# The last six blocks of a gated feed-forward's down product, as Strassen's seven products of half size

## The chip, the cores and the metric

The kernel runs on one core of a Trainium2 chip. The metric is the device time of one execution in microseconds (us). In the names below TensorE (PE) multiplies matrices and VectorE (DVE), ScalarE (ACT), GpSimd (POOL) and SyncE (SP) do the rest; SP issues nearly all transfers from HBM.

## The reference

Two decoder blocks follow each other on 512 tokens of width 1024: latent attention and two feed-forwards with windowed attention between them, and then a second block with a convolution and dilated attention. Its end is what matters here:

```python
h = rmsnorm(x, g_ffn[i])
gate = causal_dwconv3(h @ w_gate[i], ffn_conv_w[i], ffn_conv_b[i])
x = x + (jax.nn.silu(gate) * (h @ w_up[i])) @ w_down[i]        # 2816 features
ple_gate = jax.nn.sigmoid(rmsnorm(x, g_ple[i]) @ w_ple_gate[i])
x = x + ple_gate * (p[i].astype(x.dtype) @ w_ple_proj[i])
```

All is float32. 2816 features are 22 blocks of 128.

## The kernel before

Every float32 operand of a product is split in a high and a low part of a rounded format (`split`, lines 118 to 120: ScalarE casts the high part, line 119, VectorE subtracts it, line 120). `mm3` (lines 202 to 204) then does a product as three matmuls: high by high, high by low, low by high. One matmul has 128 rows of a stationary operand and up to 512 columns.

The down product of 16 of the 22 blocks is done in two passes of `down_steps`, eight blocks each. A pass cuts its hidden activations (A, 1024 features by 512 tokens) in four parts, the weights (B, 1024 by 1024) in four, and forms Strassen's seven products of half size (in Winograd's form). Sums of A and B parts are VectorE's (`a_sum`, line 915; `b_sum`, line 924), then they are split (`a_op`, `b_op`). A product fills two PSUM banks `R[0]`, `R[1]`, one for each 128 tokens of its half of the tokens. The result is added to `x` by VectorE (line 885), in one to three places. Three pairs of banks serve the seven products: the fourth product goes on in the banks of the first (`R1`), the fifth in those of the third (`R2`), the sixth in those of the second (`R3`), the seventh in `R2` again, so each of these comes behind the additions that read those banks. `down_steps` is a generator, and between its steps stand the gate and up products of later features (`gated`, 48 matmuls each), so that TensorE has other work while the sums are made.

The last six blocks' activations are split as they arise (lines 1608 and 120), and their down product is the plain one: `gemm_tm` for columns 0 to 511 and `gemm_tm_t` for 512 to 1023, four groups of 128 tokens, six blocks, three matmuls: 72 and 72. In between the second pass and it stands a small projection, `w_ple_proj` (48 matmuls), whose results ScalarE copies out of PSUM (line 1681).

When the last column half of a token group is added (`ev_down`), `to_ple` forms the last norm of these 128 tokens: a multiplication by the gain (VectorE, line 1637), squares with a running sum (ScalarE, line 1642), a square root and a few one-column operations. The transposes of that group (`put_t`, line 447) are put off by `put_off` and come after some `tick`s or when the gate product asks for them (`need`). Then `w_ple_gate` is multiplied, the end of the kernel.

The framework schedules: each engine gets its own order of instructions, from the program's order, given priorities (`tc.high_priority`) and its own cost model. On the chip each engine works in its order and waits for semaphores.

## Time and profile before

| what | us |
|---|---|
| median of 3 runs | 1692.81 (1691.04 to 1693.84) |
| the profiled execution | 1690.43 |
| its span in the profile | 1688.6 |
| TensorE busy | 1669.5 |
| VectorE busy | 1111.0 |
| ScalarE busy | 829.3 |

The span is from the first to the last instruction of the profiled execution. A line number is that of the source, often a helper's, so the names of the tiles tell more: `wr` and `wq` are raw weights, `wh` and `wl` their high and low parts, `aop` a split A operand, `r` the banks of a small product, `tm` and `tt` those of plain products, `pt` those of transposes, `hr` raw activations, `xth` and `xtl` transposed activations. Matmuls are pipelined: a row's duration is longer than the distance from the start of one to that of the next.

### The profile page before, as it was taken

The numbers are of one execution on the slowest core, as the hardware profiler recorded it, in microseconds if no ns is written. First come the engines' busy times: TensorE is split into PE (matmuls) and PEld (weight loads), VectorE is DVE, ScalarE is ACT, GpSimd is POOL, SyncE is SP. The second block draws the span as 40 slices with busy tenths as digits, with TensorE's granted clock in tenths as the row PEclk, the third lists the DMA queues.
The fourth block names the chain that finished last, engine by engine and source line by source line (L and its number), as shares of the span: only waits on it lengthen the run. The fifth ranks groups of instructions, "written<-read, shape, count | busy, mean of one in ns | idle before, by whom it ended". The sixth has DMA issues, their size and how long they took to land.

```text
span 1688.6 us, 21336 instructions
## 1 busy us (share of the span) xinstructions
PE 1669.5 (99%) x8239; PEld 1384.7 (82%) x8239; DVE 1111.0 (66%) x1938; ACT 829.3 (49%) x1416; POOL 25.6 (2%) x43
## 2 busy tenths in 40 slices
PE   8999999999999999999999999999999999999998
PEld 8777898888888877798888888988779888888887
DVE  5876648576846578738586846556765567577463
ACT  4665445444543578445444545444854343344442
POOL 0000000000001110000000000001000000000000
PEclk9999999999999999999999999999999999999999
DMA  5213244333132323413333143133352323422321
GB/s 181 69 46 130 88 150 119 100 100 100 50 125 87 101 63 119 156 50 101 101 99 100 50 126 111 39 125 99 100 187 63 88 76 99 125 63 63 113 88 63
DMA packets 125015, 165.22 MB, mean 98 GB/s; under 512 B 9385, under 2 KB 80322, under 8 KB 124914
## 3 DMA queue, kind: packets, MB, share of 16 engines
q1 hardware_dynamic: 119072, 150.03, 28.2%
q10 hardware_dynamic: 4626, 10.94, 1.9%
q0 software_dynamic: 1216, 2.89, 0.8%
q8 instruction: 65, 1.06, 0.3%
q14 instruction: 36, 0.29, 0.1%
HBM read 160.95 MB, written 2.88 MB: 97 GB/s over the span
## 4 chain that ended last, share of the span: by engine, by line
PE 94%; DVE 3%; ACT 1%; DMA 1%; issue 0%; SPq 0%; ACTq 0%; DVEq 0%
PE up L202 8%; PE up L204 8%; PE up L203 8%; PE r L202 6%; PE r L204 6%; PE r L203 6%; PE tt L203 3%; PE tt L204 3%; PE tt L202 3%; PE tm L202 2%; PE tm L203 2%; PE fm L202 2%; PE tm L204 2%; PE fm L203 2%; PE fm L204 2%; PE gp L204 2%
## 5 line engine op out<-in xcount | busy, mean ns | idle before, releaser
L120 DVE TENSOR_TENSOR wl<-wr,wh 128x1024 fp32r<-128x1024 f32 (+5 forms) x219 | 222.8, 1032 | 168.8 <-ACT wh L119 167.7
L119 ACT CAST wh<-wr 128x1024 fp32r<-128x1024 f32 (+5 forms) x219 | 193.6, 898 | 273.1 <-PE up L203 118.0
L202 PE MATMUL up<-xth,wh 128*128 128x512 f32 x608 | 236.5, 389 | 0.0
L203 PE MATMUL up<-xtl,wh 128*128 128x512 f32 x608 | 236.5, 389 | 0.0
L204 PE MATMUL up<-xth,wl 128*128 128x512 f32 x608 | 236.5, 389 | 0.0
L120 DVE TENSOR_TENSOR wl<-wq,wh 128x1024 fp32r<-128x1024 f32 x112 | 136.4, 1223 | 101.0 <-ACT wh L119 100.9
L119 ACT CAST wh<-wq 128x1024 fp32r<-128x1024 f32 x112 | 118.0, 1054 | 159.2 <-PE r L204 82.4
L204 PE MATMUL r<-wh,aop 128*128 128x512 f32 x448 | 174.3, 389 | 0.0
L202 PE MATMUL r<-wh,aop 128*128 128x512 f32 x448 | 174.3, 389 | 0.0
L203 PE MATMUL r<-wl,aop 128*128 128x512 f32 x448 | 174.3, 389 | 0.0
L204 PEld LDWEIGHTS up<-xth,wl 128*128 128x128 f32 x608 | 114.1, 188 | 23.8
L203 PEld LDWEIGHTS up<-xtl,wh 128*128 128x128 f32 x608 | 114.1, 188 | 23.6
L202 PEld LDWEIGHTS up<-xth,wh 128*128 128x128 f32 x608 | 114.1, 188 | 23.5
L204 PEld LDWEIGHTS r<-wh,aop 128*128 128x128 f32 x448 | 84.1, 188 | 17.5
L203 PEld LDWEIGHTS r<-wl,aop 128*128 128x128 f32 x448 | 84.1, 188 | 17.4
L202 PEld LDWEIGHTS r<-wh,aop 128*128 128x128 f32 x448 | 84.1, 188 | 17.4
L885 DVE SCALAR_TENSOR_TENSOR x<-x,r 128x512 f32<-128x512 f32 x144 | 92.5, 684 | 5.4 <-PE r L204 5.4
L120 DVE TENSOR_TENSOR aop<-hr,aop 128x1024 fp32r<-128x1024 f32 x56 | 67.0, 1221 | 21.5 <-ACT aop L119 21.5
L924 DVE TENSOR_TENSOR wq<-wq,wq 128x1024 f32<-128x1024 f32 x64 | 76.2, 1223 | 6.4 <-DMA wq<-in_w_down_dram 3.9
L202 PE MATMUL gp<-xth,wh 128*128 128x512 f32 x160 | 62.3, 389 | 0.0
L203 PE MATMUL gp<-xtl,wh 128*128 128x512 f32 x160 | 62.3, 389 | 0.0
L204 PE MATMUL gp<-xth,wl 128*128 128x512 f32 x160 | 62.2, 389 | 0.0
(426 smaller groups left out, 3561.4 us busy)
## 6 DMA issues: line engine op xcount, KB each, us to landing
wr<-in_mlp_w_up_dram SPq DMA_DIRECT2D x64, 512.0 KB, 3.8
wq<-in_mlp_w_down_dram SPq DMA_DIRECT2D x48, 512.0 KB, 4.3
wr<-in_w_in_dram SPq DMA_DIRECT2D x24, 512.0 KB, 3.6
wr<-in_w_gate_dram SPq DMA_DIRECT2D x22, 512.0 KB, 3.7
wr<-in_w_up_dram SPq DMA_DIRECT2D x22, 512.0 KB, 3.6
wr<-in_mlp_w_down_dram SPq DMA_DIRECT2D x16, 512.0 KB
wq<-in_w_down_dram SPq DMA_DIRECT2D x16, 512.0 KB, 7.8
wr<-in_mla_w_o_dram SPq DMA_DIRECT2D x8, 512.0 KB, 3.7
```

The source lines that it names most:

```text
L119: turned["hi"] = nc.scalar.copy(out=hi, in_=src).ins
L120: return nc.vector.tensor_tensor(out=lo, in0=src, in1=hi.bitcast(F32), op=ALU.subtract)
L202: nc.tensor.matmul(o, lhsT=sh, rhs=mh, start=start, stop=False, skip_group_check=True)
L203: nc.tensor.matmul(o, lhsT=sh, rhs=ml, start=False, stop=False, skip_group_check=True)
L204: nc.tensor.matmul(o, lhsT=sl, rhs=mh, start=False, stop=stop, skip_group_check=True)
L885: nc.vector.scalar_tensor_tensor(out=x[:, t, cs], in0=x[:, t, cs], scalar=alpha, in1=pb, op0=ALU.mult, op1=ALU.add)
L924: nc.vector.tensor_tensor(out=out[:, ks, :], in0=a[:, ks, :], in1=b[:, ks, :], op=op)
```

## The change

`down_steps` takes a number of blocks per half, `nk` (4 before, now also 3), and a function `fin` that it calls when a token group is complete. The last six blocks' activations are kept raw in two tiles of three blocks, and their down product is a third pass with `nk=3`, in place of the two plain products. No gate or up product is left to stand between its steps. The first half of the gate weights is loaded and split after the third to the sixth step (`ahead2.one()`); before, it came with the second plain product. In all passes the sums of A for the last two products now stand ahead of both, and with `fin` these two are swapped, so that token groups 0 and 1 are complete one product before 2 and 3. A `tick` follows each small product.

```diff
-    def down_steps(mb, wd, row, ra, rb, alpha, after=None):
+    def down_steps(mb, wd, row, ra, rb, alpha, after=None, nk=4, fin=None):
...
-            B[r, h] = q = mb.tile([P, 4, S], F32, tag="q", name=f"wq_{n_big[0]}")
-            for i in range(2):
-                nc.sync.dma_start(out=q[:, 2 * i:2 * i + 2, :],
-                                  in_=krows(wd, row + r * 4 + 2 * i, 2, h * 512, 512))
+            B[r, h] = q = mb.tile([P, nk, S], F32, tag="q", name=f"wq_{n_big[0]}")
+            for k0 in range(0, nk, 2):
+                kn = min(2, nk - k0)
+                nc.sync.dma_start(out=q[:, k0:k0 + kn, :], in_=krows(wd, row + r * nk + k0, kn, h * 512, 512))
...
         def product(R, a, b, start):
-            for i, (wh, wl) in enumerate(b):
+            for k0, kn, wh, wl in b:
                 for tb in range(2):
-                    for k in range(2):
+                    for k in range(kn):
                         ts_ = slice(tb * P, (tb + 1) * P)
-                        kk = 2 * i + k
+                        kk = k0 + k
                         mm3(R[tb], (a[:, 0, kk, ts_], a[:, 1, kk, ts_]), (wh[:, k, :], wl[:, k, :]),
-                            start and kk == 0, kk == 3)
+                            start and kk == 0, kk == nk - 1)
+            tick()
 
-        def add(R, th, h, al=1.0):
+        def add(R, th, h, al=1.0, last=False):
             for tb in range(2):
                 ev_add(x, al)(h, 2 * th + tb, R[tb])
+                if last and fin:
+                    fin(2 * th + tb)
...
-        b = b_op(B21)
-        product(R3, a22, b, False)
         a_sum(A12, A12, A22, ALU.subtract)
         s4 = a_op(A12)
-        add(R3, 1, 0)
-        yield
-        b = b_op(B22)
-        product(R2, s4, b, False)
-        add(R2, 0, 1)
-        yield
+        rest = [(R3, a22, B21, 1, 0), (R2, s4, B22, 0, 1)]
+        for R, a, src, th, h in reversed(rest) if fin else rest:
+            b = b_op(src)
+            product(R, a, b, False)
+            add(R, th, h, last=True)
+            yield
...
-                n_big[0] += 1
-                a = ff.tile([P, S], F32, tag="a", name=f"a_{n_big[0]}")
-                nc.vector.tensor_tensor(out=a, in0=Y.pop((gr, m)), in1=banks[m], op=ALU.mult)
-                split(*H[gr * 2 + m - 16], a)
+                M = gr * 2 + m
+                c, k = (M // 4, M % 4) if M < 16 else (4 + (M - 16) // 3, (M - 16) % 3)
+                if k == 0:
+                    RAW[c] = big("hr", F32)
+                turned["y", gr] = nc.vector.tensor_tensor(out=RAW[c][:, k, :], in0=Y.pop((gr, m)), in1=banks[m],
+                                                          op=ALU.mult).ins
...
-        gemm_tm(H, wd[16 * P:22 * P, :], [LO], ev_down)
-        ahead2 = gemm_tm_t(H, wd[16 * P:22 * P, :], [HI], ev_down, 1,
-                           nxt=lambda: ahead_tm(io["w_ple_gate_2"][0], 0, 512))
+        with pool("fl", 4) as fl:
+            ahead2 = Ahead([(krows(io["w_ple_gate_2"][0], k, 2, 0, 512), 2, 512, None) for k in range(0, 8, 2)])
+            for i, _ in enumerate(down_steps(fl, wd, 16, RAW.pop(4)[:, 0:3, :], RAW.pop(5)[:, 0:3, :], 1.0, nk=3,
+                                             fin=to_ple)):
+                if 2 <= i < 6:
+                    ahead2.one()
```

VectorE's order, before: what stands behind the small projection's four splits. `wl_1890` to `wl_1893` are parts of the down weights, `wl_1895` to `wl_1897` of the gate weights, `tm_...` banks of the plain product.

```order
L120 TENSOR_TENSOR wl_1890_13673<-wr_1890_13671,wh_1890_13672 128x1024
L120 TENSOR_TENSOR wl_1891_13707<-wr_1891_13705,wh_1891_13706 128x1024
L120 TENSOR_TENSOR wl_1892_13713<-wr_1892_13711,wh_1892_13712 128x1024
L120 TENSOR_TENSOR wl_1895_13728<-wr_1895_13726,wh_1895_13727 128x1024
L120 TENSOR_TENSOR wl_1893_13719<-wr_1893_13717,wh_1893_13718 128x1024
L120 TENSOR_TENSOR wl_1896_13734<-wr_1896_13732,wh_1896_13733 128x1024
L120 TENSOR_TENSOR wl_1897_13740<-wr_1897_13738,wh_1897_13739 128x1024
L1648 TENSOR_TENSOR x1_375_1792<-x1_375_1792,tm_1884_13607 128x512
L1648 TENSOR_TENSOR x1_375_1792<-x1_375_1792,tm_1885_13608 128x512
L1648 TENSOR_TENSOR x1_375_1792<-x1_375_1792,tm_1886_13609 128x512
L1648 TENSOR_TENSOR x1_375_1792<-x1_375_1792,tm_1887_13610 128x512
```

VectorE's order now, at the place where the fourth of the seven new products is due. `wq_1880` and `wq_1877` are the weights' parts B21 and B11, `r_1884` and `r_1885` the banks of the first product, `wl_1905` and `wl_1906` the split of B11.

```order
L924 TENSOR_TENSOR wq_1880_13599<-wq_1880_13599,wq_1877_13590 128x1024
L924 TENSOR_TENSOR wq_1880_13599<-wq_1880_13599,wq_1877_13590 128x512
L924 TENSOR_TENSOR wq_1877_13590<-wq_1878_13593,wq_1877_13590 128x1024
L924 TENSOR_TENSOR wq_1877_13590<-wq_1878_13593,wq_1877_13590 128x512
L885 SCALAR_TENSOR_TENSOR x1_375_1792<-x1_375_1792,r_1884_13613 128x512
L120 TENSOR_TENSOR wl_1905_13764<-wq_1877_13590,wh_1905_13763 128x1024
L120 TENSOR_TENSOR wl_1906_13768<-wq_1877_13590,wh_1906_13767 128x512
L885 SCALAR_TENSOR_TENSOR x1_375_1792<-x1_375_1792,r_1885_13614 128x512
L885 SCALAR_TENSOR_TENSOR x1_375_1792<-x1_375_1792,r_1884_13613 128x512
L885 SCALAR_TENSOR_TENSOR x1_375_1792<-x1_375_1792,r_1885_13614 128x512
L885 SCALAR_TENSOR_TENSOR x1_375_1792<-x1_375_1792,r_1884_13613 128x512
L885 SCALAR_TENSOR_TENSOR x1_375_1792<-x1_375_1792,r_1885_13614 128x512
```

In place of additions that stand alone there are four sums and two splits ahead of or between the six additions that read the first product's banks.

TensorE's order now, at the same place: the end of the third product (`r_1895`, `r_1896`) and the beginning of the fourth, which writes on `r_1884`. Before, the place had the plain product's matmuls.

```order
L203 MATMUL r_1895_13692<-wl_1894_13689,aop_1892_13677 128x512
L204 MATMUL r_1895_13692<-wh_1894_13688,aop_1892_13677 128x512
L202 MATMUL r_1896_13693<-wh_1894_13688,aop_1892_13677 128x512
L203 MATMUL r_1896_13693<-wl_1894_13689,aop_1892_13677 128x512
L204 MATMUL r_1896_13693<-wh_1894_13688,aop_1892_13677 128x512
L202 MATMUL r_1884_13613<-wh_1901_13723,aop_1897_13712 128x512
L203 MATMUL r_1884_13613<-wl_1901_13724,aop_1897_13712 128x512
```

The fourth product follows the third with nothing between them.

ScalarE's order, before, around the last norm: `xs_...` are squares (`xs_1907` and `xs_1908` of token group 0, `xs_1917` of group 1, `xs_1928` of 2, `xs_1940` and `xs_1941` of 3), `rs_...` roots, `xth_1900` the transposed activations.

```order
L1642 ACTIVATE xs_1928_13857,s2_1926_13854<-x1_375_1792 128x512
L1642 ACTIVATE xs_1940_13910,s2_1938_13907<-x1_375_1792 128x512
L1642 ACTIVATE xs_1908_13780,s2_1905_13775<-x1_375_1792 128x512
L424 ACT_TABLE_LOAD
L424 ACTIVATE rs_1911_13785<-rr_1910_13784 128x1
L1642 ACTIVATE xs_1918_13819,s2_1915_13814<-x1_375_1792 128x512
L424 ACTIVATE rs_1921_13824<-rr_1920_13823 128x1
L1642 ACTIVATE xs_1929_13859,s2_1926_13854<-x1_375_1792 128x512
L119 CAST xth_1900_13770<-pt_1935_13873 128x4x128
L119 CAST xth_1901_13771<-pt_1936_13880 128x4x128
L424 ACTIVATE rs_1932_13864<-rr_1931_13863 128x1
L119 CAST xth_1900_13770<-pt_1947_13926 128x4x128
```

ScalarE's order now, at the same place (`xs_1920` and `xs_1921` of group 0, `xs_1929` and `xs_1930` of 1, `xs_1942` and `xs_1943` of 2, `xs_1951` and `xs_1952` of 3).

```order
L1635 ACTIVATE xs_1920_13836,s2_1918_13833<-x1_375_1792 128x512
L119 CAST wh_1938_13880<-wq_1880_13599 128x512
L1635 ACTIVATE xs_1929_13856,s2_1927_13853<-x1_375_1792 128x512
L1635 ACTIVATE xs_1921_13838,s2_1918_13833<-x1_375_1792 128x512
L1635 ACTIVATE xs_1930_13858,s2_1927_13853<-x1_375_1792 128x512
L1635 ACTIVATE xs_1943_13909,s2_1940_13904<-x1_375_1792 128x512
L1635 ACTIVATE xs_1942_13907,s2_1940_13904<-x1_375_1792 128x512
L424 ACT_TABLE_LOAD
L424 ACTIVATE rs_1924_13843<-rr_1923_13842 128x1
L1635 ACTIVATE xs_1951_13927,s2_1949_13924<-x1_375_1792 128x512
L1635 ACTIVATE xs_1952_13929,s2_1949_13924<-x1_375_1792 128x512
L119 CAST xth_1913_13828<-pt_1959_13945 128x4x128
```

The first cast of transposed activations, of token group 0, stood behind three groups' squares and ahead of the last square of group 3; it now stands behind all eight squares.

## Rows read from the trace of the kernel before

**Rows 1.** The page: span, TensorE's share, its granted clock, the chain

```profile
span 1688.6 us, 21336 instructions
...
PE 1669.5 (99%) x8239; PEld 1384.7 (82%) x8239; DVE 1111.0 (66%) x1938; ACT 829.3 (49%) x1416; POOL 25.6 (2%) x43
...
PEclk9999999999999999999999999999999999999999
...
PE 94%; DVE 3%; ACT 1%; DMA 1%; issue 0%; SPq 0%; ACTq 0%; DVEq 0%
```

**Rows 2.** Table by stretches, old down product: length, busy us (x instructions) by engine

```profile
1602.80:1619.20 16.40, 16.40 (x74) 13.56 (x74) 6.88 (x6) 6.70 (x7) 0.00 (x0) 1.00 0.43 140
1619.20:1637.30 18.10, 18.10 (x89) 15.14 (x88) 13.67 (x33) 8.60 (x22) 0.00 (x0) 1.00 0.28 94
```

**Rows 3.** TensorE in order of time: start, us, engine, line, operation, shapes

```profile
1602.84 0.39 PE L204 MATMUL tm<-wh,ptp 128*128 128x512 f32 x1
1603.07 0.39 PE L202 MATMUL tm<-wh,ah 128*128 128x512 f32 x1
1603.30 0.39 PE L203 MATMUL tm<-wl,ah 128*128 128x512 f32 x1
...
1636.61 1.03 PE L447 MATMUL pt<-ident,xn 128*128 128x128 f32 x8
1637.40 0.48 PE L202 MATMUL tt<-wh,xth 128*128 128x512 f32 x1
```

**Rows 4.** TensorE's groups from 1580 on: x count | busy, mean ns

```profile
L202 PE MATMUL tt<-wh,ah 128*128 128x512 f32 x24 | 9.4, 393 | 0.0
...
L202 PE MATMUL tm<-wh,ah 128*128 128x512 f32 x24 | 9.3, 389 | 0.0
```

**Rows 5.** VectorE in order of time, with [idle before <-releaser]

```profile
1508.63 1.28 DVE L885 SCALAR_TENSOR_TENSOR x<-x,r 128x512 f32<-128x512 f32 x2
...
1575.39 1.23 DVE L120 TENSOR_TENSOR wl<-wq,wh 128x1024 fp32r<-128x1024 f32 x1 [0.20 <-ACT wh L119]
...
1604.84 1.23 DVE L120 TENSOR_TENSOR wl<-wr,wh 128x1024 fp32r<-128x1024 f32 x1 [4.21 <-ACT wh L119]
1609.80 2.36 DVE L120 TENSOR_TENSOR wl<-wr,wh 128x1024 fp32r<-128x1024 f32 x2 [3.74 <-ACT wh L119]
```

**Rows 6.** ScalarE's casts by shape, whole span: count | busy, mean ns

```profile
L119 ACT CAST wh<-wr 128x1024 fp32r<-128x1024 f32 x141 | 147.1, 1053 | 249.6 <-PE up L203 118.0 <-PE tm L204 37.7 <-PE r L204 30.9
...
L119 ACT CAST wh<-wr 128x512 fp32r<-128x512 f32 x58 | 34.5, 617 | 14.8 <-PE pq L203 4.5 <-PE tm L204 3.7 <-DMA wr<-in_swa_w_q_dram 2.3
...
L119 ACT CAST xth<-pt 128x512 fp32r<-128x512 f32 x56 | 30.7, 587 | 37.8 <-PE pt L447 37.4
```

**Rows 7.** The page's DMA issues: count, size, median us to landing

```profile
wq<-in_mlp_w_down_dram SPq DMA_DIRECT2D x48, 512.0 KB, 4.3
...
wq<-in_w_down_dram SPq DMA_DIRECT2D x16, 512.0 KB, 7.8
```

**Rows 8.** ScalarE in order of time, the copies out of the small projection

```profile
1599.26 0.59 ACT L1681 COPY pp<-tm 128x512 f32<-128x512 f32 x1
```

**Rows 9.** ScalarE in order of time, last norm of before

```profile
1622.32 0.62 ACT L1642 ACTIVATE xs<-x 128x512 f32<-128x512 f32 x1
...
1625.13 1.28 ACT L424 ACT_TABLE_LOAD   x1
1626.43 0.20 ACT L424 ACTIVATE rs<-rr 128x1 f32<-128x1 f32 x1
```

**Rows 10.** TensorE in order of time, the start of the program

```profile
4.75 1.94 PE L447 MATMUL pt<-ident,x 128*128 128x128 f32 x8 [4.75 <-DMA x<-in_x_dram]
...
11.52 0.57 PE L203 MATMUL tm<-wl,xth 128*128 128x320 f32 x1
11.93 0.31 PE L204 MATMUL tm<-wh,xtl 128*128 128x320 f32 x1
```

More of the change, by code (lines that the diff above doesn't have):

```diff
@@ L907, in a_op @@
             o = big("aop")
-            hl = o.rearrange("p k c -> p (k c)").rearrange("p (f k c) -> p f k c", f=2, k=4)
+            hl = o.rearrange("p k c -> p (k c)")[:, :512 * nk].rearrange("p (f k c) -> p f k c", f=2, k=nk)
             with tc.high_priority(offset=A_PRIO):
@@ L921, in b_sum @@
                     es.enter_context(tc.issue_after(after))
-                for i in range(2):
-                    ks = slice(2 * i, 2 * i + 2)
+                for k0 in range(0, nk, 2):
+                    ks = slice(k0, min(k0 + 2, nk))
                     nc.vector.tensor_tensor(out=out[:, ks, :], in0=a[:, ks, :], in1=b[:, ks, :], op=op)
@@ L927, in b_op @@
             res = []
-            for i in range(2):
+            for k0 in range(0, nk, 2):
+                kn = min(2, nk - k0)
                 n_big[0] += 1
-                wh = wp.tile([P, 1024], F32R, tag="wh", name=f"wh_{n_big[0]}")
-                wl = wp.tile([P, 1024], F32R, tag="wl", name=f"wl_{n_big[0]}")
+                wh = wp.tile([P, 1024], F32R, tag="wh", name=f"wh_{n_big[0]}")[:, :kn * 512]
+                wl = wp.tile([P, 1024], F32R, tag="wl", name=f"wl_{n_big[0]}")[:, :kn * 512]
                 with tc.high_priority(offset=B_PRIO):
-                    split(wh, wl, src[:, 2 * i:2 * i + 2, :].rearrange("p k c -> p (k c)"))
-                res.append([t.rearrange("p (k c) -> p k c", k=2) for t in (wh, wl)])
+                    split(wh, wl, src[:, k0:k0 + kn, :].rearrange("p k c -> p (k c)"))
+                res.append((k0, kn) + tuple(t.rearrange("p (k c) -> p k c", k=kn) for t in (wh, wl)))
             return res
         def product(R, a, b, start):
-            for i, (wh, wl) in enumerate(b):
+            for k0, kn, wh, wl in b:
                 for tb in range(2):
-                    for k in range(2):
+                    for k in range(kn):
                         ts_ = slice(tb * P, (tb + 1) * P)
-                        kk = 2 * i + k
+                        kk = k0 + k
                         mm3(R[tb], (a[:, 0, kk, ts_], a[:, 1, kk, ts_]), (wh[:, k, :], wl[:, k, :]),
-                            start and kk == 0, kk == 3)
-        def add(R, th, h, al=1.0):
+                            start and kk == 0, kk == nk - 1)
+            tick()
+        def add(R, th, h, al=1.0, last=False):
             for tb in range(2):
                 ev_add(x, al)(h, 2 * th + tb, R[tb])
+                if last and fin:
+                    fin(2 * th + tb)
         def banks2(n):
@@ L1572, in tile_hybrid_decoder @@
     with pool("ff", 2) as ff:
-        H = []
         RAW = {}
@@ L1595, in up_ev @@
         def up_ev(gr, banks):
-            if gr < 8 and gr % 2 == 0:
-                RAW[gr // 2] = big("hr", F32)
-            elif gr % 2 == 0:
-                hh, hl = big("ah"), big("al")
-                H.extend((hh[:, m, :], hl[:, m, :]) for m in range(4 if gr < 10 else 2))
-            for m in range(2):
-                if gr < 8:
-                    turned["y", gr] = nc.vector.tensor_tensor(
-                        out=RAW[gr // 2][:, gr % 2 * 2 + m, :], in0=Y.pop((gr, m)), in1=banks[m], op=ALU.mult).ins
-                    continue
-                n_big[0] += 1
-                a = ff.tile([P, S], F32, tag="a", name=f"a_{n_big[0]}")
-                nc.vector.tensor_tensor(out=a, in0=Y.pop((gr, m)), in1=banks[m], op=ALU.mult)
-                split(*H[gr * 2 + m - 16], a)
+            for m in range(2):
+                M = gr * 2 + m
[4 more added lines that the diff above has]
+                                                          op=ALU.mult).ins
         def gated(gr, part):
@@ L1644, in to_ple @@
             nc.vector.tensor_copy(rple[:, t:t + 1], rsqrt(ss, 1, 1.0 / D, RMS_EPS))
-        def ev_down(gi, t, pb):
-            cs = slice(gi * 512, gi * 512 + 512)
-            nc.vector.tensor_tensor(out=x[:, t, cs], in0=x[:, t, cs], in1=pb, op=ALU.add)
-            if gi == 1:
-                to_ple(t)
         gated_first()
```

## The prediction

> **What bounds the kernel now.** I read the page first, then the table by stretches, then TensorE's, VectorE's and ScalarE's instructions in order of time over the last 100 us, which is where the change lies. The page: TensorE is busy 99% of 1688.6 us, its granted clock is full in all 40 slices, and 94% of the chain that ended last is TensorE [rows 1]. The stretches: over the old down product of the last six blocks TensorE is busy in the whole of 16.40 and 18.10 us, while VectorE has 6.88 and 13.67 us of work [rows 2]. In order of time its matmuls follow each other every 0.227 us, from 1603.07 to the last transposes at 1636.61, and the product with the gate weights starts at 1637.40 without a gap [rows 3]. So a matmul that is taken away is worth its 0.227 us, as long as the other engines deliver; VectorE has 14 us free in these 34.
>
> **What is removed.** The old product has 6 groups of 24 matmuls, 144 in all [rows 4]; the new one has 7 products of 3 blocks, 2 token blocks and 3 terms, 126. TensorE's order has 18 rows less, so the change does what it says. 18 x 0.2268 = 4.1 us off TensorE. The 33.5 us from 1603.07 to 1636.61 are 144 x 0.2268 = 32.7 and one set of eight transposes, 0.87, so nothing else was in them.
>
> **What is added, and where it stands.** All A and B sums and splits of the small products, and 18 additions to x in place of 8. These are VectorE's and ScalarE's, and they stand in a fixed order. One 128x1024 split or sum costs VectorE 1.23 us alone and 1.13 in a row (2.36 for two), a 128x512 addition 0.60 in a row (1.28 for two) [rows 5]. The new 128x768 form is not in the trace: it lies between 0.60 and 1.13; as its width lies halfway I take 0.87, and keep 0.27 either way for each. ScalarE's cast is 1.05 for 1024 and 0.62 for 512 columns [rows 6]; 0.84 for 768. On the way to this place I cost the change at nothing: the loads leave when the last split of the second pass's weights is done, at 1576.6 [rows 5]: 3 MB, which at 4 to 8 us for a landing [rows 7] are there by about 1590; the earlier passes only have two steps swapped, with 48 matmuls of other work around each.
>
> The old chain of casts in the small projection ahead is the start. ScalarE casts the first A operand after its fifth copy out of that projection (start 1599.26, 0.59) [rows 8]: 1599.85 + 0.84 = 1600.7. From there VectorE's queue is never empty.
>
> *First wait.* The first product's result is added to x three times, six instructions, and its two banks are then written on by the fourth product. In VectorE's new order the last of the six stands 27th from the first A split: 9 of 768 columns, 6 of 1024, 12 of 512. 9 x 0.87 + 6 x 1.13 + 12 x 0.60 = 21.8 us. Ahead of the split of B21 it waits for ScalarE, whose 16 instructions to there take 6 x 0.84 + 3 x 0.59 + 2 x 0.62 + 5 x 1.05 = 13.3, to 1613.1, while VectorE is there after 9 x 0.87 + 2 x 1.13 + 2 x 0.60 = 11.3, at 1612.0: 1.1 more. The banks are free at 1600.7 + 21.8 + 1.1 = 1623.6. TensorE is through three products at 1603.07 + 54 x 0.2268 = 1615.3 (their operands are split in time: the last is done near 1611.5 and wanted at 1614). **It waits 8.3 us.**
>
> *Second and third.* The fifth product writes on the third's banks, whose two additions come 7 instructions later: 2 x 1.13 + 0.87 + 4 x 0.60 = 5.5, 1629.1. TensorE is there at 1623.6 + 4.1 = 1627.7: **1.4 us**. TensorE's order then mixes the last two products, and the third matmul there needs the split of the changed B21, six instructions on: 3 x 1.13 + 3 x 0.60 = 5.2, 1634.3, and TensorE is there at 1629.1 + 4.1 and two matmuls, 1633.6: **0.7 us**. The other 34 matmuls end at 1634.3 + 7.7 = 1642.0, the eight transposes of token block 0 at 1642.9.
>
> *Fourth.* Before, token block 0 was transposed a group of 18 matmuls ahead of its use. Now all four blocks come at the end, and ScalarE's cast of block 0 stands behind the squares of all four. The sixth product ends ten matmuls ahead, 1639.8; then on VectorE two additions, two 1024-wide multiplications and an addition: 3 x 0.60 + 2 x 1.13 and some 0.3 of small ones, 1644.2. On ScalarE a square of 0.62, the table load of 1.28, a root of 0.20, two squares [rows 9], and the cast of 0.59 [rows 6]: 3.9, so 1648.1. **TensorE waits 5.2 us.** If this cover were as before, the wait would be nothing.
>
> Sum without the clock: -4.1 + 8.3 + 1.4 + 0.7 + 5.2 = +11.5 us. The same from the ends: 1648.1 against 1637.40, and one set of transposes, 0.87, more to come.
>
> *The clock.* In these waits TensorE stands still. The page shows its full level throughout, but its record begins after the start: there eight transposes take 1.94 us against 1.03 at 1636.61, and a 320-column matmul 0.57 at 11.52 but 0.31 at 11.93 [rows 10]. So from the first instruction at 4.75, after idling, to 11.9 it ran at the lower of its two levels, 1.2 GHz, for 7.1 us. How long an idle time in the middle costs it the upper level, no row shows. At the low end: nothing. At the high end both long waits do, each as at the start, and half of 7.1 is lost after each: 3.6 after the fourth, and after the first 3.6 less the 2.1 us that TensorE would wait anyway: 5.1 together. I take 1.5, the longer wait alone, since it is clearly longer than the 4.75 of idling that the start shows.
>
> The Trainium skill (TensorE: Matmul & The Clock Gate, "HAM oscillation — how this bites in real kernels") says that waits between bursts of matmuls put the array back to half rate and that each burst then starts slow, which speaks against any change that trades matmuls for pauses. By that page the sum would hold both prices, near its upper end; the start of this trace agrees as far as it goes, and no row shows a pause in the middle.
>
> **The forecast.** +11.5 + 1.5 = +13.0. The profiled execution took 1690.43 us for its span of 1688.6; it would be 1703.4. The median of the runs, 1692.81, is 2.4 above it, so the time measured in the same way is 1705.8.
>
> **The rivals.**
> - *VectorE keeps up, and the kernel is faster.* This is the place of the first wait: if the six additions were over by 1615.3, and block 0 were ready by the last product, all of the 4.1 us would be won: 1688.7. For it: VectorE has more than 9 us free of 16.4 in the first stretch [rows 2], and between its splits it idles 3 to 5 us [rows 5]. Against: the 27 instructions would have to fit into 14.6 us instead of 21.8, 0.54 on average, which is less than even a 512-wide one takes. The point from which it decides is VectorE's total: 14.6 us. 4%.
> - *No wait for the banks.* The same wait stands in every pass of before, and TensorE never shows it [rows 1]. If the order of the additions were no bound, -4.1 + 1.4 + 0.7 + 5.2 = +3.2: 1696.0. Against: there, 48 matmuls or 10.9 us of another product lie between the steps, and here nothing. 10%.
> - *The clock falls in both waits*, with the price of its high end: +11.5 + 5.1 = +16.6, 1709.4. For it: the start. Against: 5.2 us hardly exceed the 4.75 of the start, and there are transposes in that wait. 18%.
> - *The weights come late.* All eight loads wait in SP's queue for one split at 1576.6, and a sum in VectorE's queue waits for them, with the last up product's multiplication behind it. There are some 4 us to spare before the projection's second half is late; 5 us beyond that would give 1711. The bursts of before landed in 7.8 us at the median [rows 7], so 5%.
>
> **How the numbers follow.** The forecast has 63%. Its own range is 1702 to 1708: ten 768-wide instructions at 0.27 less and no fall of the clock give 11.5 - 2.7 = +8.8, at 0.27 more and with the clock's 1.5 they give +15.7; the middle of that is likelier than its ends. The range of 8 in 10 reaches to the clock's rival and takes in the late weights, and leaves out the first and the second rival, 14%: 1699 to 1711. A measurement of this kernel can tell about 0.2%, 3.4 us, from no change. Faster: the first rival, 4%. Within 0.2%: half of the second, 5%. Slower: 91%.
>
> **What would show it.** In the profile after: 18 matmuls less, TensorE idle 7 to 10 us in one piece ahead of the fourth small product, put down to VectorE's additions to x; two waits of 1 to 2 us; VectorE without a gap for some 35 us from 1600.7; then 4 to 6 us ahead of the gate product, put down to ScalarE's cast. A clock below full in one or two stretches after the waits would set the last term. The prediction is wrong if the first wait is under 4 us, if VectorE shows gaps between the A splits and the last addition, or if a wait stands elsewhere, in the passes ahead for one.

## The result, and the profile after

The changed kernel takes 1703.3 us (median of 4 runs, 1701.99 to 1707.63), the kernel before 1693.05 beside it (4 runs, 1691.04 to 1693.84): a ratio of 1.0067, interval 1.0047 to 1.0087, or 10.2 us slower. The forecast was 1705.8, the range 1699 to 1711.

From the page of the changed kernel, its lines that answer to [rows 1]:

```profile
span 1705.3 us, 21351 instructions
...
PE 1674.1 (98%) x8221; PEld 1386.7 (81%) x8221; DVE 1134.4 (67%) x1969; ACT 835.4 (49%) x1425; POOL 25.6 (2%) x43
...
PEclk9999999999999999999999999999999999999989
...
PE 91%; DVE 5%; DMA 2%; ACT 2%; issue 1%; SPq 0%; ACTq 0%; DVEq 0%
```

TensorE has 18 matmuls less and VectorE 23.4 us more to do; the last slice but one shows a lower clock, and VectorE now has 5% of the chain. TensorE in order of time, which answers to [rows 3], with the idle time ahead of a row and its releaser in brackets:

```profile
1627.30 0.77 PE L202 MATMUL r<-wh,aop 128*128 128x512 f32 x1 [6.86 <-DVE x L885]
1627.86 0.63 PE L203 MATMUL r<-wl,aop 128*128 128x512 f32 x1
1628.29 0.63 PE L204 MATMUL r<-wh,aop 128*128 128x512 f32 x1
...
1632.13 0.50 PE L204 MATMUL r<-wh,aop 128*128 128x512 f32 x1
1632.47 0.39 PE L202 MATMUL r<-wh,aop 128*128 128x512 f32 x1
...
1639.15 0.50 PE L203 MATMUL r<-wl,aop 128*128 128x512 f32 x1 [0.56 <-DVE wl L120]
...
1646.97 1.03 PE L447 MATMUL pt<-ident,xn 128*128 128x128 f32 x8
1652.60 0.62 PE L202 MATMUL tt<-awh,xth 128*128 128x512 f32 x1 [4.60 <-ACT xth L119]
```

Here stand the wait ahead of the fourth product (6.86), a small one where the sixth and seventh mix (0.56), and the wait ahead of the gate product (4.60). Behind each long one the matmuls start 0.43 us apart instead of 0.227, and the table by stretches (length, busy us and instructions of PE, PEld, DVE, ACT, POOL, then the granted clock, the share and rate of the DMAs) tells why:

```profile
1620.40:1627.30 6.90, 0.04 (x2) 0.03 (x1) 6.90 (x11) 2.30 (x3) 0.00 (x0) 0.87 0.00 0
1627.30:1632.10 4.80, 4.80 (x11) 3.78 (x12) 4.80 (x7) 0.00 (x0) 0.00 (x0) 0.50 0.34 106
...
1647.80:1652.60 4.80, 0.20 (x2) 0.00 (x0) 4.45 (x14) 3.95 (x11) 0.00 (x0) 1.00 0.00 0
1652.60:1656.40 3.80, 3.80 (x10) 2.80 (x11) 3.00 (x16) 0.94 (x4) 0.00 (x0) 0.55 0.00 0
```

The clock is at 0.50, 1.2 GHz, behind the first wait and nearly so behind the last. VectorE was busy through the whole first wait. Its queue, in order of time, which answers to [rows 5]:

```profile
1605.63 2.70 DVE L120 TENSOR_TENSOR aop<-hr,aop 128x768 fp32r<-128x768 f32 x3 [0.47 <-ACT aop L119]
1608.36 0.96 DVE L915 TENSOR_TENSOR hr<-hr,hr 128x768 f32<-128x768 f32 x1
...
1618.79 3.56 DVE L924 TENSOR_TENSOR wq<-wq,wq 128x1024 f32<-128x1024 f32 x4
1622.27 0.68 DVE L885 SCALAR_TENSOR_TENSOR x<-x,r 128x512 f32<-128x512 f32 x1
1622.93 1.83 DVE L120 TENSOR_TENSOR wl<-wq,wh 128x1024 fp32r<-128x1024 f32 x2
1624.68 3.07 DVE L885 SCALAR_TENSOR_TENSOR x<-x,r 128x512 f32<-128x512 f32 x5
```

From 1605.63 on no row has an idle time ahead of it until 1633.80 (0.52); the six additions of the first product to x come last, at 1622.27 and from 1624.68 on. ScalarE ahead of the gate product, which answers to [rows 9]:

```profile
1648.62 0.63 ACT L1635 ACTIVATE xs<-x 128x512 f32<-128x512 f32 x1 [1.66 <-DVE x L885]
...
1649.36 1.28 ACT L424 ACT_TABLE_LOAD   x1
...
1651.38 0.61 ACT L1635 ACTIVATE xs<-x 128x512 f32<-128x512 f32 x1
...
1651.99 0.56 ACT L119 CAST xth<-pt 128x512 fp32r<-128x512 f32 x1
```

The cast that TensorE waits for stands behind squares, table load and root. TensorE's matmuls up to the small projection are the same in both kernels and in the same order, but this one execution ran 4.7 us late before it came to the change: its first projection matmul, the second fence, against the same of before, the first; the third is a row of the changed kernel's table by stretches:

```profile
1592.04 0.50 PE L202 MATMUL tm<-wh,ptp 128*128 128x512 f32 x1 [0.58 <-ACT ptp L119]
```

```profile
1596.73 0.50 PE L202 MATMUL tm<-wh,ptp 128*128 128x512 f32 x1
```

```profile
75.00:90.00 15.00, 12.79 (x47) 8.71 (x48) 9.52 (x27) 7.83 (x20) 0.00 (x0) 0.77 0.20 57
```

From 75 to 90 us its clock was 0.77 (3.4 us lost; before it was 1.00 there), and at the start it came up 2.6 us later, which cost 1.2 us. This execution was the slowest of the four, 1707.63; the others are 3.8 to 5.6 below it. So the two profiles are compared from that matmul on: 1688.6 - 1592.04 = 96.6 us to the end of the span before, 1705.3 - 1596.73 = 108.6 after, 12.0 more. The rows add up to it: -4.1 + 6.9 + 0.6 + 4.6, and 12 and 8 matmuls each 0.2 too long, 4.1, are 12.1.

### The profile page after: what moved, and what is told of

Read it like the earlier page. It is cut to its first block, busy times and chain, and to the rows that moved or that the text cites. A ratio compares the mean times of both kernels' runs of the same rounds, so it can differ in the third digit from the quotient of the medians.

```text
span 1705.3 us, 21351 instructions
## 1 busy us (share of the span) xinstructions
PE 1674.1 (98%) x8221; PEld 1386.7 (81%) x8221; DVE 1134.4 (67%) x1969; ACT 835.4 (49%) x1425; POOL 25.6 (2%) x43
## 4 chain that ended last, share of the span: by engine, by line
PE 91%; DVE 5%; DMA 2%; ACT 2%; issue 1%; SPq 0%; ACTq 0%; DVEq 0%
PE up L204 8%; PE up L202 8%; PE up L203 8%; PE r L203 6%; PE r L202 6%; PE r L204 6%; PE fm L202 2%; PE fm L204 2%; PE fm L203 2%; PE tt L203 2%; PE tt L202 2%; PE tt L204 2%; PE gp L204 2%; PE gp L202 2%; PE gp L203 2%; PE tm L204 2%
## 5 line engine op out<-in xcount | busy, mean ns | idle before, releaser
L119 ACT CAST wh<-wr 128x1024 fp32r<-128x1024 f32 (+5 forms) x209 | 183.4, 890 | 273.7 <-PE up L203 127.0
L120 DVE TENSOR_TENSOR wl<-wr,wh 128x1024 fp32r<-128x1024 f32 (+5 forms) x209 | 211.0, 1023 | 154.7 <-ACT wh L119 153.9
L120 DVE TENSOR_TENSOR wl<-wq,wh 128x1024 fp32r<-128x1024 f32 x126 | 149.4, 1193 | 103.8 <-ACT wh L119 103.7
L119 ACT CAST wh<-wq 128x1024 fp32r<-128x1024 f32 x126 | 129.6, 1030 | 180.1 <-PE r L204 99.3
L202 PE MATMUL r<-wh,aop 128*128 128x512 f32 x490 | 191.6, 391 | 6.9 <-DVE x L885 6.9
L203 PE MATMUL r<-wl,aop 128*128 128x512 f32 x490 | 191.7, 391 | 0.6 <-DVE wl L120 0.6
L204 PE MATMUL r<-wh,aop 128*128 128x512 f32 x490 | 191.3, 391 | 0.0
L202 PEld LDWEIGHTS r<-wh,aop 128*128 128x128 f32 x490 | 92.5, 189 | 26.6 <-issue 7.3
L885 DVE SCALAR_TENSOR_TENSOR x<-x,r 128x512 f32<-128x512 f32 x162 | 103.9, 683 | 8.2 <-PE r L204 8.2
L204 PEld LDWEIGHTS r<-wh,aop 128*128 128x128 f32 x490 | 92.5, 189 | 19.3
L120 DVE TENSOR_TENSOR aop<-hr,aop 128x1024 fp32r<-128x1024 f32 (+1 forms) x63 | 73.3, 1191 | 21.7 <-ACT aop L119 21.7
L119 ACT CAST aop<-hr 128x1024 fp32r<-128x1024 f32 (+1 forms) x63 | 62.4, 1024 | 2.7 <-DVE hr L915 1.9
```

The source lines that it names most:

```text
L119: turned["hi"] = nc.scalar.copy(out=hi, in_=src).ins
L120: return nc.vector.tensor_tensor(out=lo, in0=src, in1=hi.bitcast(F32), op=ALU.subtract)
L202: nc.tensor.matmul(o, lhsT=sh, rhs=mh, start=start, stop=False, skip_group_check=True)
L203: nc.tensor.matmul(o, lhsT=sh, rhs=ml, start=False, stop=False, skip_group_check=True)
L204: nc.tensor.matmul(o, lhsT=sl, rhs=mh, start=False, stop=stop, skip_group_check=True)
L885: nc.vector.scalar_tensor_tensor(out=x[:, t, cs], in0=x[:, t, cs], scalar=alpha, in1=pb, op0=ALU.mult, op1=ALU.add)
```

## The experiments

All are variants of the changed kernel but the first, which is one of the kernel before. Times are medians; "above" and "below" are against runs of the kernel before on the same chip (1691.2 to 1691.6), the ratios have their interval. The changed kernel itself is 10.2 above, but the kernel before beside it took 1693.05, 1.5 to 1.9 us more than beside the experiments. So a difference from the changed kernel is given a second time where it matters, from the profiled executions: the time from the first projection matmul to the end of the span, 96.6 us before and 108.6 in the changed kernel.

### Do the rewritten passes ahead cost anything?

```diff
+            tick()
...
+        a_sum(A12, A12, A22, ALU.subtract)
+        s4 = a_op(A12)
         b = b_op(B21)
         product(R3, a22, b, False)
-        a_sum(A12, A12, A22, ALU.subtract)
-        s4 = a_op(A12)
```

> The kernel before with one part of the change alone: in the two kinds of passes of four blocks the last two products are built in the new loop, with the count of the tick behind every product; the last six blocks stay the plain down product. My theory (all of the 10.2 us is lost behind the first projection matmul): 1693.1 us, within 0.2% of the kernel before. Rival (the rewritten passes ahead cost something of their own, by a changed place of the transfers or of the additions): over 2 us more than before, with TensorE's waits in the passes ahead longer.

1691.63 us, 0.5 above; ratio 1.0002 (0.9992 to 1.0012). The rewritten passes ahead cost nothing that can be told from zero. What this kernel leaves as it was, the activations kept raw and the earlier loads, costs nothing up to the first projection matmul either: apart from the clock in the two places above, the changed kernel is there as early as before. So the loss is the third pass and what stands behind it.

### The first wait: the order of VectorE's work, or its amount?

```diff
-        for th, h in ((0, 1), (1, 0), (1, 1)):
-            add(R1, th, h, alpha)
+        with tc.high_priority(offset=2 * A_PRIO if fin else 0):
+            for th, h in ((0, 1), (1, 0), (1, 1)):
+                add(R1, th, h, alpha)
```

> The changed kernel with the six additions of the first product to x put ahead of the sums and splits in VectorE's queue (a higher priority, in the last pass alone). Theory O (the fourth product waits only because of the order in which VectorE takes up its work): the 6.9 us ahead of the fourth product go with the 2.4 us at the lower clock behind them, no wait of over 2 us takes their place, and the time is 1694 us (1692 to 1696). Theory V (VectorE has more work for the first four products than TensorE's own three products last, in whatever order): the fourth product starts without a wait, and the fifth waits 8 to 11 us for its operands; the time is 1701 to 1704 us, at most 2 us from the changed kernel's. I hold V.

```diff
-        for th, h in ((0, 1), (1, 0), (1, 1)):
+        for th, h in ((0, 1), (1, 0), (1, 1)) + (((0, 0),) if fin else ()):
             add(R1, th, h, alpha)
...
-        product(R1, a12, b, False)
+        if fin:
+            R4 = banks2("r")
+            product(R4, a12, b, True)
...
-        add(R1, 0, 0, alpha)
+        add(R4, 0, 0, alpha)
```

> The changed kernel with the fourth product of the last pass in a pair of banks of its own, so that it doesn't wait for the first product's additions; its own sums are then added to x by themselves (two additions of 128 x 512 more). Theory O (the wait is for the banks alone): the wait goes and the time is 1694 to 1697 us. Theory V (VectorE's work is too much for the stretch): the fourth product starts at once, and a wait of 10 to 13 us stands ahead of the fifth, longer than the one that went, since VectorE has two additions more; the time is 1702 to 1706 us. I hold V.

With the additions first: 1700.14, 9.0 above, ratio 1.0056 (1.0041 to 1.0071). With banks of its own for the fourth product: 1701.39, 10.2 above, 1.0063 (1.0048 to 1.0078). TensorE's long row in the Strassen pass, of the first and of the second:

```profile
1631.68 0.77 PE L202 MATMUL r<-wh,aop 128*128 128x512 f32 x1 [9.60 <-DVE x L885]
```

```profile
1630.76 0.77 PE L202 MATMUL r<-wh,aop 128*128 128x512 f32 x1 [11.26 <-DVE x L885]
```

The fourth product goes without a wait in both, and the fifth waits 9.60 and 11.26 us, as V told. (In absolute times both are under V's ranges, by 0.9 and 0.6 us.) Moving the wait gives back little: TensorE's waits from the projection on are 10.9 and 12.6 us in sum, against 12.1 in the changed kernel. The wait ahead of the gate product is 1.1 us at its longest in both, and no slow matmuls stand behind it; TensorE comes to it later, and ScalarE's order ahead of it differs too, which these runs don't part. By the profiled executions 2.8 and 1.0 us are had back.

The other side is to take work away and leave the order:

```diff
+                    if fin:
+                        nc.scalar.copy(out=wh, in_=src[:, k0:k0 + kn, :].rearrange("p k c -> p (k c)"))
+                        wl = wh
```

> The changed kernel, in whose last pass VectorE does not form the low parts of the weight combinations (the matmuls take the high part in their place: the count of matmuls and their operands' sizes are as they were, but the low part of the weights is left out of the result). VectorE has some 12 us less to do in the pass, TensorE the same. Theory V (VectorE's amount of work sets the waits of the Strassen pass): the 6.9 us ahead of the fourth product fall to 2 to 3 us, no wait of over 3 us stands ahead of a later product, and the time is 2 to 5 us above the kernel before (the wait ahead of the gate product stays, 2 to 5 us). Rival (the banks' hand-over or the order is what is waited for, whatever VectorE's amount): the wait stays above 5 us and the time 8 us or more above the kernel before.

1691.57 us, the time of the kernel before: ratio 0.9999 (0.9989 to 1.0008), 2 us better than I had expected. (With `wl = wh` the high part enters the result a second time; the matmuls are as many as before.) A stretch of 22.2 us around the end of the wait, of the changed kernel and of this one, this one's row of the wait, and VectorE's first row in its pass:

```profile
1605.60:1627.80 22.20, 15.34 (x67) 12.47 (x66) 22.14 (x28) 14.94 (x20) 0.00 (x0) 0.95 0.07 24
```

```profile
1595.00:1617.20 22.20, 21.11 (x94) 17.16 (x93) 15.88 (x20) 18.35 (x26) 0.00 (x0) 1.00 0.08 24
```

```profile
1617.16 0.47 PE L202 MATMUL r<-wh,aop 128*128 128x512 f32 x1 [1.09 <-DVE x L885]
```

```profile
1601.25 2.70 DVE L120 TENSOR_TENSOR aop<-hr,aop 128x768 fp32r<-128x768 f32 x3 [6.53 <-ACT aop L119]
```

VectorE falls from 22.14 to 15.88 busy us in the stretch; from its first A split (1605.63, here 1601.25) to the start of the fourth product (1627.30, here 1617.16) it is 21.7 and 15.9. The wait falls from 6.86 to 1.09, and the clock stays up. So it is VectorE's amount of work, against the time that TensorE has work of its own up to there. The wait ahead of the gate product is 1.7 here, less than the 2 to 5 that I had told.

### The wait ahead of the gate product

```diff
-                                             fin=to_ple)):
+                                             fin=lambda t: to_ple(t) if t < 2 else late.append(t))):
...
+        need(("xt", 0))
+        for t in late:
+            to_ple(t)
```

> The changed kernel with one order altered: the squares of the third and fourth token blocks are taken up by ScalarE behind the cast of the first token block's turned copy, and no longer ahead of it. My theory (the wait of 4.6 us ahead of the gate product is ScalarE's queue, and the 8 to 9 matmuls at the lower clock behind it cost some 1.7 us): the wait falls under 1 us, the stretch at the lower clock behind it goes too, and the time is 1697 us (1695.5 to 1698.5). Rival (the cast waits for the last additions and their root, or the wait comes back ahead of a later token block's matmuls): 1701 us or more, with a wait of over 3 us somewhere behind the eight transposes. The wait of 6.9 us in the Strassen pass stays in both.

1696.21 us, 5.1 above, ratio 1.0034 (1.0021 to 1.0048); 5.2 less than the changed kernel. The cast on ScalarE and what now stands behind it, and on TensorE the gate product's first matmul:

```profile
1644.20 0.58 ACT L119 CAST xth<-pt 128x512 fp32r<-128x512 f32 x1 [0.65 <-PE pt L447]
1645.22 0.63 ACT L1635 ACTIVATE xs<-x 128x512 f32<-128x512 f32 x1 [0.43 <-DVE x L885]
```

```profile
1644.84 0.50 PE L202 MATMUL tt<-awh,xth 128*128 128x512 f32 x1 [0.24 <-ACT xth L119]
```

The cast now waits only for the transposes; TensorE waits 0.24 and then runs at 0.227. By the profiled executions 5.8 us are had back (102.8 from the first projection matmul on): 4.4 of this wait, and the rest, 1.4, is near the 1.7 of the slow matmuls behind it. So this wait was an order and nothing else. The edit moves the whole norms of the two blocks, the table load on ScalarE and two 1024-wide multiplications on VectorE with the squares, so the share of the squares alone is not shown. Half of the loss could be had by a few lines.

### The clock's own price

```diff
+        def fill(n):
+            pb = bank("fill")
+            for j in range(n):
+                nc.tensor.matmul(pb, lhsT=pth[:, 0, 0:P], rhs=pth[:, 1, :], start=j == 0, stop=j == n - 1)
...
+                if i == 2:
+                    fill(28)
...
+        need(("xt", 0))
+        fill(18)
```

> The changed kernel with matmuls that nobody reads in the two long waits: 28 of 128 x 512 behind the third product (6.4 us at 0.227) and 18 behind the eight transposes (4.1 us). TensorE then has no long idle time there. If the lower clock behind both waits is what TensorE's idleness brings, the granted clock stays at the upper level to the end; the matmuls behind come at 0.227 us; the time falls by the price of the clock alone. From the rows of the changed kernel that is 12 matmuls and 8 to 9 at 0.427 in place of 0.227, or 4.1 us, less what the later products then wait for VectorE (up to 1.6 us): 1.5 to 4 us less than the changed kernel, or 6 to 8.5 us above the kernel before. Rival (the clock falls there for another reason, or the price was hidden in the waits): the changed kernel's time within 1 us, 9 to 11 us above the kernel before.

1700.03 us, 8.5 above, ratio 1.0051 (1.0036 to 1.0066): 1.7 less than the changed kernel, at the low end of what I expected and under 0.2%, so the time alone would not settle it. The clock does: stretches behind the first and the second filling, and the row of the transposes:

```profile
1621.50:1628.30 6.80, 6.48 (x29) 4.86 (x27) 6.50 (x10) 3.36 (x4) 0.00 (x0) 1.00 0.47 147
...
1646.80:1650.00 3.20, 3.20 (x18) 2.66 (x17) 2.40 (x17) 0.41 (x2) 0.00 (x0) 1.00 0.00 0
```

```profile
1641.78 1.09 PE L447 MATMUL pt<-ident,xn 128*128 128x128 f32 x8 [1.47 <-DVE xn L1630]
```

With TensorE kept busy the clock stays at its upper level behind both places. The price of the clock can't be read from the time, though, since the other engines' orders changed with the edit. Four of the six additions on VectorE, the cast on ScalarE, and TensorE's second filling:

```profile
1616.32 2.48 DVE L885 SCALAR_TENSOR_TENSOR x<-x,r 128x512 f32<-128x512 f32 x4
```

```profile
1642.47 0.58 ACT L119 CAST xth<-pt 128x512 fp32r<-128x512 f32 x1
```

```profile
1642.62 4.36 PE L1672 MATMUL fill<-ptp 128*128 128x512 f32 x18
```

The additions are over at 1618.80, 2.7 us before the first filling ends (1621.49), and the cast, now ahead of the table load, at 1643.05, 3.8 us before the gate product starts (1646.82). So in this order the unread matmuls, and not the old waits, held TensorE at least for a part of both places. The rows give this kernel's time from the first projection matmul on as 46 unread matmuls, 10.4 us, and 2.8 of waits, less the 4.1 saved: 9.1 above before, where the profiled executions show 9.3 (105.8). What the waits would have been in this order, with the upper clock and without the filling, no run shows; so the clock's net price stays open. Its gross price is the 4.1 us of slow matmuls; of the second fall's share some 1.4 us came back in time by the late squares (5.8 less 4.4 of wait).

### Both together

Two of the edits above, the high parts alone and the late squares, in one kernel:

```diff
+                        wl = wh
...
+        need(("xt", 0))
+        for t in late:
+            to_ple(t)
```

> The kernel that leaves the low parts of the weight combinations out of the last pass and so out of the result, with the squares of the third and fourth token blocks behind the first block's cast as well. With the first of the two alone the time was that of the kernel before, with 1.4 us of waits in the pass, 1.7 us ahead of the gate product and 0.4 at its next piece. Theory (the 18 removed matmuls are worth 4.1 us of time wherever nothing waits): the wait ahead of the gate product falls under 0.6 us and the time is 1 to 3 us below the kernel before. Rival (the removed matmuls give nothing, and the time is held by VectorE's or ScalarE's chain in any case): within 0.7 us of the kernel before.

1689.3 us, 2.3 below, ratio 0.9987 (0.9978 to 0.9997). Its longest waits are 1.09 in the pass and 0.24 ahead of the gate product. The two waits, with what they do to the clock, are the whole loss: without them the removed matmuls do show, 4.1 us less the 1.6 of waits that are left (1.4 in the pass, 0.2 behind it).

### Other work for TensorE in the waits

```diff
-        gemm_tm([(pth[:, k, :], pth[:, 2 + k, :]) for k in range(2)], io["w_ple_proj_2"][0], [LO, HI],
-                lambda gi, t, pb: nc.scalar.copy(out=pp[gi][:, t, :], in_=pb))
...
+        plan, left = [0, 0, 2, 1, 2, 0, 0, 0], [(gi, t) for gi in range(2) for t in range(NB)]
...
+                proj(plan[i + 1])
...
+        proj(max(len(left) - 2, 0))
+        need(("xt", 0))
+        proj(len(left))
```

> The changed kernel with the eight pieces of the projection (6 matmuls of the token block each) spread over the pass: two behind the second product, one behind the third, two behind the fourth, one at the end, and two behind the transposes of the first token block, where TensorE waited. Theory (the waits can be filled with TensorE's own work, since VectorE only lags by some 7 us): no wait above 4 us in the pass, the wait ahead of the gate product under 2.5 us, and the time 4 to 7 us above the kernel before. Rival (VectorE starts as much later as its work is the same, so what is filled here is missing as lead in front of the pass): the waits are as long as before in sum, and the time stays 9 us or more above the kernel before.

1696.55 us, 5.0 above, ratio 1.0029 (1.0018 to 1.004), in the range. Then with other places, the gate weights' splits a product later, and the late squares:

```diff
+        plan, left = [0, 0, 3, 1, 2, 1, 1, 0], [(gi, t) for gi in range(2) for t in range(NB)]
...
-                if 2 <= i < 6:
+                proj(plan[i + 1])
+                for _ in range((3, 4, 5, 6).count(i)):
                     ahead2.one()
...
+        for t in late:
+            to_ple(t)
```

> The changed kernel with no arithmetic moved to another engine and none left out, only its order: the eight pieces of the projection are spread over the pass (three behind the second product, one, two and one behind the next, one behind the sixth), the splits of the gate product's weights come one product later, and the squares of the third and fourth token blocks behind the first block's cast. It takes both orders that helped by themselves. Theory (VectorE is behind by a bounded amount, which TensorE's own later and earlier work can cover): no wait over 2.2 us, the upper clock to the end, and the time 0 to 3 us above the kernel before; the 4.1 us of removed matmuls are then eaten by waits of 4 to 6 us in sum. Rival (waits come back elsewhere when both orders meet): 4 us or more above.

1691.28 us, 0.3 below, ratio 1.0001 (0.9991 to 1.001). It computes all of the reference and has had back what the change cost, but no more. Its waits behind 1590 us (total, times, longest):

```profile
PE tm L202 <- ACT pp L1678: 1.3, 1, 1.3
PE r L202 <- ACT aop L119: 0.9, 1, 0.9
PE r L202 <- ACT wh L119: 0.7, 1, 0.7
PE tt L202 <- ACT xth L119: 0.5, 2, 0.2
PE r L204 <- DVE aop L120: 0.5, 1, 0.5
```

3.9 us in sum, just under the 4 to 6 that I had told, against 4.1 of matmuls saved. VectorE has the same work as in the changed kernel: what it could not do in time is covered here by TensorE's own work, put where TensorE waited.

### GpSimd as a helper

```diff
+            eng = nc.gpsimd if fin and nsum[0] in (0, 1, 2, 3) else nc.vector
...
-                    nc.vector.tensor_tensor(out=out[:, ks, :], in0=a[:, ks, :], in1=b[:, ks, :], op=op)
+                    eng.tensor_tensor(out=out[:, ks, :], in0=a[:, ks, :], in1=b[:, ks, :], op=op)
...
+            low[0] = nc.gpsimd if fin and nb[0] in (3, 5) else None
```

> The woven projection of the run above, and with it the four sums of weight blocks and the low parts of the fourth and sixth products' weights formed by GpSimd in the last pass (some 12 instructions of 128 x 1024 or 128 x 512, 6.3 us less on VectorE). Theory V with free GpSimd: all waits under 1.5 us each, the time within 2 us of the kernel before, perhaps 1 us below. Rival G (GpSimd takes over 2.6 us for 128 x 1024, or VectorE gets slower beside it): products wait for GpSimd's sums, and the time is 4 us or more above the kernel before.

1700.24 us, 8.7 above, ratio 1.0047 (1.0031 to 1.0064): 3.7 us more than the woven projection alone, my rival G. TensorE's longest wait is 5.4 us, for VectorE's additions; for GpSimd's own results it waits 1.0. As VectorE was slow in places where nothing of GpSimd's was waited for, the next run gave GpSimd work that nobody reads:

```diff
+        spare = fs.tile([P, 2, S], F32, name="spare")
+        for _ in range(10):
+            nc.gpsimd.tensor_tensor(out=spare, in0=pp[0][:, 2:4, :], in1=pp[0][:, 2:4, :], op=ALU.add)
```

> The changed kernel with ten additions of 128 x 1024 on GpSimd that nobody reads, beside the last pass (from about the end of the projection on, some 22 to 30 us). Nothing waits for them. Theory G (VectorE's two-operand instructions get slower while GpSimd computes, as the run with the sums on GpSimd suggests: a split of 128 x 1024 took 3.42 us beside it and 1.22 without): VectorE's instructions in the stretch take 1.3 to 3 times as long, the wait ahead of the fourth product grows from 6.9 to over 12 us, and the time is 17 us or more above the kernel before. Rival (what was slow there was waiting for GpSimd's own results): VectorE's instructions keep their 1.22 and 0.95 us, and the time stays 9 to 12 us above the kernel before.

1718.68 us, 27.1 above, ratio 1.016 (1.0143 to 1.0177). VectorE's groups from 1600 to 1650 us (count | busy us, mean ns) of the changed kernel:

```profile
L120 DVE TENSOR_TENSOR aop<-hr,aop 128x768 fp32r<-128x768 f32 x7 | 6.4, 953 | 0.5 <-ACT aop L119 0.5
...
L915 DVE TENSOR_TENSOR hr<-hr,hr 128x768 f32<-128x768 f32 x2 | 1.9, 955 | 0.0
```

The same groups of the run with the unread additions, and GpSimd's own:

```profile
L120 DVE TENSOR_TENSOR aop<-hr,aop 128x768 fp32r<-128x768 f32 x7 | 14.3, 2080 | 0.5 <-ACT aop L119 0.5
...
L915 DVE TENSOR_TENSOR hr<-hr,hr 128x768 f32<-128x768 f32 x2 | 5.2, 2589 | 0.0
```

```profile
L1672 POOL TENSOR_TENSOR spare<-pp 128x1024 f32<-128x1024 f32 x10 | 24.8, 2484 | 360.5 <-ACT pp L1668 359.8
```

The same sum of 128 x 768 takes 2589 ns instead of 955, about as long as one GpSimd instruction (2484). The waits came in other places than I had told: 11.7 us ahead of the second matmul of the third product, for a split, and the one ahead of the fourth is 7.0, hardly longer than before. So GpSimd is no way to lighten VectorE here.

## Why the prediction was right

- *The removed matmuls, -4.1:* 8221 against 8239, and 2.3 us of it can be measured once the two long waits are gone (*Both together*).
- *First wait, +8.3; it was 6.9.* The mechanism is as told: place, releaser, VectorE without a gap. Its start was 0.2 us off (1605.63, against 1600.7 moved by the 4.7 us of the late execution). Two small things are missing: ScalarE never held VectorE up (the 1.1 us), since its casts of 768 columns come 0.74 apart in a row and I took 0.84; and the fourth product started when five of the six additions were done, 0.6 sooner. Here the cost of the unmeasured form, 0.87, was right: three took 2.70 with 0.96 for one alone.
- *Second and third, +1.4 and +0.7; there was 0.6.* While TensorE ran at half rate behind the first wait, VectorE had that time to catch up; in the kernel with unread matmuls, where the clock stayed up, 2.8 us of waits stood there, though in another order. The prediction had this trade only in its upper clock case.
- *Fourth, +5.2; it was 4.6.* The gate product was to start at 1648.1 + 4.7 = 1652.8 and did at 1652.60. That it is an order, and can be changed, the late squares showed.
- *Clock, +1.5; the rows have 4.1.* This is the term that was mis-sized. It fell behind both waits and not only behind the longer one, though the second, 4.60, was shorter than the 4.75 of idling at the start by which the prediction chose. So the rival's mechanism came true, but not its price of 5.1: 12 slow matmuls, 2.4 us, and 8, 1.7. Part of that was probably hidden, since the two small waits behind the first fall were 1.5 us shorter than forecast; the net price no run shows. The Trainium skill's rule that the prediction weighed ("TensorE: Matmul & The Clock Gate", "HAM oscillation — how this bites in real kernels"), by which waits between bursts of matmuls make the next burst start slow, agrees with both falls (granted clock 0.50 and 0.55 behind them); the upper end of the sum, +16.6, to which the prediction took it, was too high.
- *The sum:* +13.0 told, +12.0 in the profile. That it is so close is in part luck: the four waits came out 3.6 us shorter than told, the clock's rows 2.6 longer. The other 1.5 us between 1705.8 and 1703.3 are the anchor: I added the 2.4 us by which the profiled execution of before lay under its median, and the changed kernel's, less the 4.7 it lost early, lies 0.4 under; against that, its time outside the span is 0.5 longer.
- *The passes ahead at nothing:* right, by the first experiment. *VectorE keeps up* and *no wait for the banks* are out by the runs on order and amount; the latter would have given 1696.0, and fresh banks gave 10.2 above. *Late weights:* none of TensorE's waits there names a load. VectorE did wait 2.96 us for one, up to 1591.27, but then idled 3.10 more before its split at 1603.93, so it cost nothing that shows.

## What to carry to other kernels

Strassen takes matmuls from TensorE and gives additions to VectorE; in a pass with no other product between its steps, count VectorE's instructions up to each bank that is used again, and compare with TensorE's time up to there. A long wait that is due to an engine's amount of work only moves when that engine's work is reordered, while one that is due to an order (the squares ahead of the cast) is had back by changing a few lines: take the work away in one run and reorder it in another, and the two tell themselves apart. A wait of the first kind can still be covered by other work of TensorE's own, as the woven projection did, if there is any to move there. Where TensorE waits, price what comes behind too, but only as far as the other engine doesn't catch up in that time. An edit that only fills a wait can change the other engines' orders as well: look in its trace whether what was waited for still comes as late.

## What was not expected of the hardware

- VectorE and GpSimd get into each other's way even where neither waits for the other, but not with every instruction. Two of VectorE's rows and one of GpSimd's from the kernel with the sums on GpSimd:

```profile
1610.43 1.87 DVE L887 SCALAR_TENSOR_TENSOR x<-x,r 128x512 f32<-128x512 f32 x3
...
1613.53 3.42 DVE L122 TENSOR_TENSOR awl<-wr,awh 128x1024 fp32r<-128x1024 f32 x1
```

```profile
1609.77 6.09 POOL L930 TENSOR_TENSOR wq<-wq,wq 128x1024 f32<-128x1024 f32 x2
```

  All start beside GpSimd's two sums. The split, with both operands in SBUF, takes 3.42 us instead of 1.22; the three additions, with one operand in PSUM, take 0.62 each as ever. The Trainium skill ("SBUF — State Buffer", "SBUF: two separate sides") says that the two engines share a pair of ports as an exclusive lock, which a VectorE instruction with two SBUF inputs takes, for its whole length, against a GpSimd instruction that reads SBUF; the one that starts later waits. The trace agrees: the split ends at 1616.95, 1.09 us behind the end of GpSimd's second sum (1615.86), about as long as it takes alone.
- The clock can fall without one long wait. In the first woven kernel it fell behind waits of 1.40, 0.89 and 2.13 us, which end at 1613.40, 1618.89 and 1623.58. In its successor, with waits of 1.28, 0.67 and 0.24 us in the same part, its mean over the execution is 1.000. The stretches of the former, the clock being the third number from the end:

```profile
1612.00:1619.00 7.00, 4.71 (x21) 3.60 (x21) 7.00 (x10) 3.62 (x5) 0.00 (x0) 1.00 0.23 75
1619.00:1624.00 5.00, 2.87 (x12) 2.09 (x13) 5.00 (x7) 3.51 (x6) 0.00 (x0) 1.00 0.54 162
1624.00:1628.00 4.00, 4.00 (x12) 3.10 (x11) 3.23 (x5) 0.41 (x1) 0.00 (x0) 0.57 0.56 176
```
